# Storing the first-stage gate blocks raw, with their silu moved to the channel stage, and a new place for the residual's first tile

## The chip, the cores and the metric

The kernel runs on one core of one Trainium2 chip. The metric is the device time of one execution in microseconds (us). Engines are named as in the profile: PE is TensorE's matrix multiply and PEld its weight load, DVE is VectorE, ACT is ScalarE, POOL is GpSimd, and SP is the engine whose queue issues every transfer (DMA) of this kernel. L405 is line 405 of the kernel before.

## The reference

The kernel computes two layers of a hybrid decoder on a sequence of 1024 tokens of width 1024, in float32. One layer is:

```
h    = rms_norm(x, norm_g)
proj = h @ w_in
q_lat, kv_lat, k_rope, g_mla, c_h, c_b, c_c, g_conv, s_q, s_k, s_v, g_swa = split(proj)
y_mla  = mla_mixer(q_lat, kv_lat, k_rope, ...)   * silu(g_mla)     # latent attention, causal
y_conv = c_b * causal_conv3(c_c * c_h)           * silu(g_conv)    # short depthwise convolution
y_swa  = swa_mixer(s_q, s_k, s_v, ..., sinks)    * silu(g_swa)     # window of 128, softmax with sinks
x      = x + concat(y_mla, y_conv, y_swa) @ w_out
```

The change touches `silu(g_mla)`, the values that are kept until the latent attention is done, and the start of `x + ... @ w_out`.

## The kernel before

Every float32 product is made as three matmuls of a split pair (a rounded high part and the rest): high by high, high by low, low by high. `mm3` writes out these three for each block of 128 of the contraction, at L188, L189 and L190. Weights are loaded raw and split into such pairs (L171 makes the high part, L173 the low part; L551 and L552 in the channel stage). A buffer named `wraw` holds a raw piece, `whi` and `wlo` the pair; there are three raw buffers and eight pairs.

A layer runs in these stages, one behind the other on TensorE:

- **First stage.** The window attention runs in 16 steps (two halves of heads by eight blocks of 128 tokens). A step makes scores, masks them on VectorE (L353), takes exp on ScalarE (L358), scales on GpSimd (L364), transposes (L374), copies (L375) and multiplies with the values (L384). Between its parts the function `fill` puts other units: eight `unit_b` and eight `unit_a` (latents; the lists `P1_FILL` say how many at each step), then the gate blocks `unit_m`: a 128 by 512 block of `g_mla`, transposed, goes through silu on ScalarE (L405) into a buffer `gt` and by a transfer into the DRAM buffer `gm_d` (L406). Six of the eight `unit_m` of a layer run in this stage. The pool `p1` holds its tiles; `ali`, the mask of 4 KB per partition, is the first of them.
- **Channel stage.** The other two `unit_m` and the eight `unit_s` come first. Then the convolution's channels are made in four pairs of groups (`group_u` and `group_g`), each a scheme of seven products instead of eight (`seven`, L587) on sums and differences of quarters of the weights (`quarters`, with the tiles `a12` and `asum`) and of the input (`t_a`, `t_b`, `t_c`). The pool `cp` holds a ring of five buffers `st` of 2 KB per partition, `a12`, `asum` and three `yv`. `group_g` applies silu (L625), multiplies, and stores its result to DRAM as `ycv_d` (L649). DVE instructions of a group follow one another in a fixed order (`in_turn`). The last group calls two functions on the way (`beside`): `split_y` splits the window attention's result (blocks 4 to 7) and the convolution's (blocks 0 to 3) into the pairs `yh` and `yl` (L674, L676). Blocks 0 to 2 are loaded back from `ycv_d` as `yr`; block 3 is still in `yv`.
- **Output stage.** `unit_o` multiplies the pairs with `w_out` in 32 units of 24 matmuls (L188 to L190, here on `whi`, `yh`), over three PSUM buffers, and adds the residual tile `xr` (L723). `load_x` loads four blocks of it at a time into a ring of three buffers of 4 KB (tag `pt`) of the pool `at`, whose memory lies where `cp` was. From the unit numbered 9 on, `lat_t` transposes the latents (L741), which were stored to `lat_d` in the first stage and are loaded back by one transfer of 1.66 MB (L703).
- **Attention stage.** The latent attention runs in the same way with exp (L933), multiplies its rows by the stored gate (`gm`, loaded from `gm_d` during the output stage), and the last product and the next layer's norm follow.

The order of instructions on each engine is made by the framework's planner: it takes the program in the order in which it is written as priority, keeps a timeline of its own, and puts on each engine what is ready by that timeline. Within `tc.issue_after(i)` an instruction is put behind `i` on the same engine. A tile that reuses memory of a closed pool waits for the tiles that lay there (`reuse_waits="tile"`). An engine, and the SP queue, takes its instructions in order, so a wait holds all that is behind it.

Of the kernel before, what the change touches and what calls it, by code (L numbers as in the profile page):

```python
# [10 lines left out]
F32 = mybir.dt.float32  # L11
# [8 lines left out]
P = 128  # L20
# [43 lines left out]
def f32(ap):  # L64
    return ap.bitcast(F32)
# [3 lines left out]
def trunk(ctx, tc, x, norm_g, w_in, w_qb, w_kvb, w_out, c_gain, c_rope, c_idb, c_ali, out):  # L69
# [115 lines left out]
    def mm3(o, pairs):  # L185
        n = len(pairs)
        for i, (lh, ll, rh, rl) in enumerate(pairs):
            pe.matmul(o, lhsT=lh, rhs=rh, start=(i == 0), stop=False)  # L188
            pe.matmul(o, lhsT=lh, rhs=rl, start=False, stop=False)  # L189
            pe.matmul(o, lhsT=ll, rhs=rh, start=False, stop=(i == n - 1))  # L190

# [52 lines left out]
    for l in range(depth):  # L244
# [157 lines left out]
        def unit_m(w, k, hf, tmp):  # L402

            gt = tmp()
            s.activation(out=gt, in_=chan_mm(w, k % 2 * P, hf), func=AF.Silu)  # L405
            nc.sync.dma_start(out=gm_d[:, k, hf * 512:hf * 512 + 512], in_=gt)  # L406

        def unit_s(w, k, hf, tmp):
# [29 lines left out]
        units += [(lambda t=t: unit_a(t, W["a"])) for t in range(NT)]  # L438
        tmp = [lambda: p1.tile([P, 512], F32, name="gt", tag="gt", bufs=1)]
        for f, o in ((unit_m, O_GM), (unit_s, O_GS)):  # L440
            for jj in range(2):
                units += [(lambda f=f, k=2 * jj + c, hf=hf: f(W["gate"], k, hf, tmp[0])) for hf in (1, 0) for c in range(2)]
        after = {NT - 1: ("a", [win[:, :, O_QL:O_QL + QL], win[:, :, O_KR:O_KR + RD]])}
# [55 lines left out]

        tmp[0] = st  # L500
        tt = [a16(f"T{n}", FR).rearrange("p (b k q) -> p b k q", b=2, k=4) for n in range(3)]
# [7 lines left out]

        def whole(n, k):  # L510
            return sub(st(), f32(qx[n][0][:, k]), f32(qx[n][1][:, k]), ALU.add)

# [5 lines left out]
        def t_a(k):  # L518
            a, b = whole(4, k), whole(1, k)
            t2[k] = a, sub(b, a, b)  # L520
            t_split(5, k, b)
# [114 lines left out]
        def group_g(j, beside=(), e=g):  # L636
            yv = [cp.tile([P, 512], F32, name="yv", tag="yv", bufs=3) for _ in range(2)]
            kept.update(enumerate(yv))
            for hf in range(2):
                conv(j, hf, yv[hf])  # L640

            def times(hf, a, e):
                if e is v:
                    in_turn(yv[hf], a, yv[hf], ALU.mult)
                else:
                    e.tensor_tensor(out=yv[hf], in0=a, in1=yv[hf], op=ALU.mult)

            def store(hf):
                nc.sync.dma_start(out=ycv_d[:, j, hf * 512:hf * 512 + 512], in_=yv[hf])  # L649

            def last(o, a):
                times(1, plus(o, a), e)
                store(1)

            def c21(o, a):
                times(0, silu(o, a), e)
                store(0)

            seven(O_CB + j * P, O_GC + j * P, lambda o: times(0, o, v), c21, lambda o, a: times(1, silu(o, a), e), last, None, beside)
# [31 lines left out]
        for f, j in ((group_g, 0), (group_u, 1), (group_g, 1), (group_u, 2), (group_g, 2), (group_u, 3)):  # L691
            f(j)
        marks["turn"] = None
        group_g(3, (lambda: split_y(0, range(4, 8)), lambda: split_y(0, range(4))), v)

# [5 lines left out]
        kr = latf[:, NT * 384:NT * 416].rearrange("p (t c) -> p t c", t=NT)  # L701
        with tc.issue_after(marks["raw"].ins):
            nc.sync.dma_start(out=latf[:, :NT * 416], in_=lat_d)  # L703
        close(cp_cm)
# [7 lines left out]
        def load_x(qd, hf):  # L712
            xq[qd, hf] = at.tile([P, 4, 256], F32, name="xr", tag="pt", bufs=3)
            cs = slice(qd * 256, qd * 256 + 256)
            nc.sync.dma_start(out=xq[qd, hf], in_=xin[hf * 512:hf * 512 + 512, cs].rearrange("(t p) c -> p t c", p=P))

        def unit_o(qd, t, w):
            o = ps_g()[:, :256]
            hf, c = t // 4, (t % 4) * P
            yh, yl = y12[hf]  # L720
            mm3(o, [(yh[:, k, c:c + P], yl[:, k, c:c + P], *w[k]) for k in (4, 5, 6, 7, 0, 1, 2, 3)])
            xr = xq[qd, hf]
            v.tensor_tensor(out=xr[:, t % 4], in0=o, in1=xr[:, t % 4], op=ALU.add)  # L723
            if t % 4 == 3:
                cs = slice(qd * 256, qd * 256 + 256)
                nc.sync.dma_start(out=x1p[hf * 512:hf * 512 + 512, cs].rearrange("(t p) c -> p t c", p=P), in_=xr)
# [10 lines left out]
        def lat_t(k, hf):  # L737
            gn = kag[:, l:l + 1] if k == 2 else qag[:, l, k:k + 1]
            tp = ps_t()
            for c in range(4):  # L740
                pe.transpose(tp[:, c * P:(c + 1) * P], lat[:, hf * 4 + c, k * P:(k + 1) * P], idn)  # L741
            dst = slice(hf * 512, hf * 512 + 512)
# [269 lines left out]
        for i in range(4):  # L1012
            start += [lambda i=i: k1(0, i), lambda i=i: q1(0, 2 * i), lambda i=i: q1(0, 2 * i + 1), lambda i=i: k2(0, i)]
        load_x(0, 0)
        w1, wlp, wl, xTn, last = None, [], [], {}, []
# [181 lines left out]
```

## Time and the profile before

| | us |
|---|---|
| median of 3 runs (lowest, highest) | 1598.77 (1594.41, 1599.61) |
| the profiled execution | 1596.56 |
| its span, from the first to the last instruction | 1594.7 |

The profile and its trace are of that one execution. Busy time is summed per engine; TensorE's matmuls are pipelined, so a busy TensorE is not one at its peak. Idle time before an instruction is put down to the instruction that released it. PEclk is the granted clock of TensorE as a share of the full one. Of the stretches in the rows below, 65 to 260 lies in the first stage of layer 0 (its gate blocks from 164 on), 313 to 460 in its channel stage, 460 to 485 at the turn to its output stage; 850 to 1060 and 1246 to 1272 are the like places of layer 1.

### The profile page before, as it was taken

To read this page: it belongs to the slowest core of one execution; us is meant where nothing else is said; L and a number is where in the kernel's file an instruction comes from. 1 tells how busy PE (TensorE), PEld (TensorE's weight loads), DVE (VectorE), ACT (ScalarE), POOL (GpSimd) and SP (SyncE) were. 2 spreads that over 40 slices of the span, in tenths; PEclk is the share of its full clock that TensorE was granted. 3 is DMA by queue.
4 is the path that set the end of the run, shared out by engine and by line. 5 is a ranking of instruction groups with operands and counts; after the bars stand their busy time and mean duration, and the time that the engine had idled before them with its cause. 6 is when DMAs were issued, how large, how long until landed. Compare 5 with 4: busy or idle time off the path is not lost.

```text
span 1594.7 us, 25470 instructions
## 1 busy us (share of the span) xinstructions
PE 1495.8 (94%) x9084; PEld 1319.6 (83%) x9084; DVE 1102.9 (69%) x2197; ACT 739.9 (46%) x1763; POOL 734.8 (46%) x960
## 2 busy tenths in 40 slices
PE   6899988999999999999989998899999899999998
PEld 5898877788879998888778897778888799888887
DVE  6765565876774668887656755668667756788964
ACT  4353554422230258886524445644222302688851
POOL 6444231544434655874245423314444356568640
PEclk9999999999999999999999999999999999999999
DMA  6100222122246610013241102211222564100123
GB/s 203 34 10 21 83 67 60 27 60 64 82 139 209 208 51 2 1 41 121 79 134 33 29 1 81 75 54 39 70 77 60 190 206 152 47 1 14 47 75 131
DMA packets 116641, 122.73 MB, mean 77 GB/s; under 512 B 16417, under 2 KB 102305, under 8 KB 115746
## 3 DMA queue, kind: packets, MB, share of 16 engines
q1 hardware_dynamic: 116514, 121.10, 24.7%
q8 instruction: 72, 1.18, 0.3%
q14 instruction: 55, 0.45, 0.1%
HBM read 92.50 MB, written 28.57 MB: 76 GB/s over the span
## 4 chain that ended last, share of the span: by engine, by line
PE 74%; DVE 8%; ACT 8%; issue 4%; DMA 3%; POOL 3%; SPq 0%; POOLq 0%; ACTq 0%; DVEq 0%
PE ps_g L188 13%; PE ps_g L189 12%; PE ps_g L190 12%; PE ps_b L587 8%; PE ps_a L587 5%; PE ps_c L587 5%; PE ps_s L920 4%; PE ps_g L964 4%; PE ps_s L349 2%; ACT apr L933 2%; PE ps_g L384 2%; PE ps_t L950 1%; PE ps_t L374 1%; DVE pt L959 1%; DMA wraw<-in_w_in_dram 1%
## 5 line engine op out<-in xcount | busy, mean ns | idle before, releaser
L173 POOL TENSOR_TENSOR wlo<-wraw,whi 128x512 fp32r<-128x512 f32 (+2 forms) x120 | 164.8, 1380 | 134.5 <-DVE whi L171 98.8
L188 PE MATMUL ps_g<-whi,xh 128*128 128x320 f32 (+2 forms) x512 | 161.3, 315 | 5.9 <-ACT pr L358 1.8
L190 PE MATMUL ps_g<-whi,xl 128*128 128x320 f32 (+2 forms) x512 | 159.3, 311 | 0.0
L189 PE MATMUL ps_g<-wlo,xh 128*128 128x320 f32 (+2 forms) x512 | 159.2, 311 | 0.0
L190 PE MATMUL ps_g<-whi,yl 128*128 128x256 f32 x512 | 146.9, 287 | 5.6 <-DVE yl L676 5.6
L188 PE MATMUL ps_g<-whi,yh 128*128 128x256 f32 x512 | 147.6, 288 | 3.3 <-DVE xr L723 2.8
L189 PE MATMUL ps_g<-wlo,yh 128*128 128x256 f32 x512 | 145.9, 285 | 0.0
L964 PE MATMUL ps_g<-pt,vs 128*128 128x256 f32 (+1 forms) x640 | 120.6, 300 | 13.9 <-DVE pt L959 8.9
L364 POOL TENSOR_SCALAR pr<-pr,sri 128x256 f32<-128x256 f32 (+1 forms) x128 | 59.0, 479 | 140.7 <-DVE sri L362 108.7
L171 DVE CAST whi<-wraw 128x512 fp32r<-128x512 f32 (+2 forms) x128 | 82.0, 647 | 48.6 <-DMA wraw<-in_w_out_dram 22.5
L964 PEld LDWEIGHTS ps_g<-pt,vs 128*128 128x128 f32 x640 | 91.4, 190 | 25.6 <-DVE pt L959 15.1
L959 DVE TENSOR_TENSOR pt<-ps_t,pt 128x512 fp32r<-128x512 f32 (+1 forms) x160 | 100.2, 632 | 16.1 <-ACT pt L958 13.9
L188 PEld LDWEIGHTS ps_g<-whi,xh 128*128 128x128 f32 x512 | 102.4, 200 | 7.6 <-issue 2.7
L920 PE MATMUL ps_s<-kt,qh 96*128 96x512 f32 (+3 forms) x384 | 106.2, 361 | 0.9
L936 POOL TENSOR_SCALAR apr<-apr,ari 128x896 f32<-128x896 f32 (+2 forms) x80 | 71.7, 896 | 75.2 <-DVE ari L935 64.0
L190 PEld LDWEIGHTS ps_g<-whi,yl 128*128 128x128 f32 x512 | 99.2, 194 | 7.0 <-DVE yl L676 7.0
L188 PEld LDWEIGHTS ps_g<-whi,yh 128*128 128x128 f32 x512 | 99.3, 194 | 5.1 <-DVE xr L723 4.1
L189 PEld LDWEIGHTS ps_g<-wlo,xh 128*128 128x128 f32 x512 | 102.0, 199 | 1.6
L924 DVE TENSOR_REDUCE am<-ps_s 128x1 f32<-128x128 f32 (+7 forms) x128 | 95.6, 750 | 9.5 <-PE ps_s L922 7.1
L190 PEld LDWEIGHTS ps_g<-whi,xl 128*128 128x128 f32 x512 | 101.7, 199 | 0.4
L958 ACT CAST pt<-ps_t 128x512 fp32r<-128x512 f32 (+1 forms) x160 | 85.7, 542 | 35.2 <-PE ps_g L190 17.9
L188 PE MATMUL ps_g<-xh,whi 128*128 128x512 f32 x256 | 101.0, 395 | 0.0
(245 smaller groups left out, 4503.0 us busy)
## 6 DMA issues: line engine op xcount, KB each, us to landing
wraw<-in_w_in_dram SPq DMA_DIRECT2D x104, 256.0 KB, 2.9
wraw<-in_w_out_dram SPq DMA_DIRECT2D x80, 256.0 KB, 3.0
x1p<-xr SPq DMA_DIRECT2D x16, 512.0 KB, 3.2
p<-x1p SPq DMA_DIRECT2D x16, 512.0 KB, 3.5
x<-in_x_dram SPq DMA_DIRECT2D x8, 512.0 KB, 5.1
a<-in_w_in_dram SPq DMA_DIRECT2D x16, 256.0 KB, 3.4
ycv_d<-yv SPq DMA_DIRECT2D x16, 256.0 KB, 2.7
xr<-in_x_dram SPq DMA_DIRECT2D x8, 512.0 KB, 4.7
```

The lines of the kernel that those rows point to most:

```text
L171: cast(out=hi, in_=raw)
L173: e.tensor_tensor(out=lo, in0=raw, in1=f32(hi), op=ALU.subtract)
L188: pe.matmul(o, lhsT=lh, rhs=rh, start=(i == 0), stop=False)
L189: pe.matmul(o, lhsT=lh, rhs=rl, start=False, stop=False)
L190: pe.matmul(o, lhsT=ll, rhs=rh, start=False, stop=(i == n - 1))
L587: pe.matmul(o, lhsT=a[:, k], rhs=b[:, k], start=(first and k == 0 and i == 0), stop=(k == 3 and i == 2), skip_group_check=True)
L920: pe.matmul(sp[:, kk], lhsT=a[:, hs], rhs=kt[0:QK, b, h, kk], start=(ai == 0), stop=(ai == 2 and c0 + w < n))
L924: v.tensor_reduce(out=m, in_=sp[:, :n], axis=AX.X, op=ALU.max)
L936: g.tensor_scalar(out=pr[:, :n], in0=pr[:, :n], scalar1=ri, scalar2=1.0, op0=ALU.mult, op1=ALU.mult)
L958: s.copy(out=pt[:, 0, lo_c:], in_=tp[:, lo_c:])
L959: v.tensor_tensor(out=pt[:, 1, lo_c:], in0=tp[:, lo_c:], in1=f32(pt[:, 0, lo_c:]), op=ALU.subtract)
L964: pe.matmul(av[:, q0:], lhsT=vb, rhs=pt[:, a, q * 256 + q0:(q + 1) * 256], start=(bb == 0 and bi == 0 and a == 0), stop=(last and bi == 1 ...
```

## The change

`unit_m` copies a gate block raw while the first stage runs and notes it in the list `m_raw`; once the channel stage's buffers exist it applies silu as before. The new function `silu_m` loads one noted block from `gm_d` into a buffer of the ring `st`, applies silu in place, and stores it back; it is called once behind each of six groups of the channel stage. `a12` and `asum` become the first tiles of the pool `cp`: they are made ahead of everything else in it, and the first `t_a` uses them for its two sums. The first `load_x` is called as soon as the pool `at` is open, ahead of every other tile of it, so that its tile is the first there; the load of the latents is put behind it. The transposes of `lat_t` are put behind the last matmul of the latest `unit_o` (`mm3` now returns it). The convolution's block 3 is no longer stored to `ycv_d`. The first of the two functions beside the last group now also splits blocks 0 and 1, the second blocks 2 and 3.

```diff
--- before.py
+++ after.py
@@ -187,7 +187,8 @@
         for i, (lh, ll, rh, rl) in enumerate(pairs):
             pe.matmul(o, lhsT=lh, rhs=rh, start=(i == 0), stop=False)
             pe.matmul(o, lhsT=lh, rhs=rl, start=False, stop=False)
-            pe.matmul(o, lhsT=ll, rhs=rh, start=False, stop=(i == n - 1))
+            r = pe.matmul(o, lhsT=ll, rhs=rh, start=False, stop=(i == n - 1))
+        return r
 
     def rsqrt(name, ss, w, scale, eps):
         g.tensor_scalar(out=ss, in0=ss, scalar1=scale, scalar2=eps, op0=ALU.mult, op1=ALU.add)
@@ -402,8 +403,21 @@
         def unit_m(w, k, hf, tmp):
 
             gt = tmp()
-            s.activation(out=gt, in_=chan_mm(w, k % 2 * P, hf), func=AF.Silu)
+            o = chan_mm(w, k % 2 * P, hf)
+            if len(tmps) > 1:
+                s.activation(out=gt, in_=o, func=AF.Silu)
+            else:
+                s.copy(out=gt, in_=o)
+                m_raw.append((k, hf))
             nc.sync.dma_start(out=gm_d[:, k, hf * 512:hf * 512 + 512], in_=gt)
+
+        def silu_m():
+            k, hf = m_raw.pop(0)
+            gt = st()
+            blk = gm_d[:, k, hf * 512:hf * 512 + 512]
+            nc.sync.dma_start(out=gt, in_=blk)
+            s.activation(out=gt, in_=gt, func=AF.Silu)
+            nc.sync.dma_start(out=blk, in_=gt)
 
         def unit_s(w, k, hf, tmp):
 
@@ -436,10 +450,11 @@
 
         units = [(lambda t=t: unit_b(t, W["b"])) for t in range(NT)]
         units += [(lambda t=t: unit_a(t, W["a"])) for t in range(NT)]
-        tmp = [lambda: p1.tile([P, 512], F32, name="gt", tag="gt", bufs=1)]
+        m_raw = []
+        tmps = [lambda: p1.tile([P, 512], F32, name="gt", tag="gt", bufs=1)]
         for f, o in ((unit_m, O_GM), (unit_s, O_GS)):
             for jj in range(2):
-                units += [(lambda f=f, k=2 * jj + c, hf=hf: f(W["gate"], k, hf, tmp[0])) for hf in (1, 0) for c in range(2)]
+                units += [(lambda f=f, k=2 * jj + c, hf=hf: f(W["gate"], k, hf, tmps[-1])) for hf in (1, 0) for c in range(2)]
         after = {NT - 1: ("a", [win[:, :, O_QL:O_QL + QL], win[:, :, O_KR:O_KR + RD]])}
         for n, o in enumerate((O_GM, O_GM + 256, O_GS, O_GS + 256)):
             after[2 * NT - 1 + 4 * n] = n, [win[:, :, o:o + 256]]
@@ -497,7 +512,7 @@
             return cp.tile([P, 512], F32, name="st", tag="st", bufs=5)
 
 
-        tmp[0] = st
+        tmps.append(st)
         tt = [a16(f"T{n}", FR).rearrange("p (b k q) -> p b k q", b=2, k=4) for n in range(3)]
         qx = {n: tuple(x[:, 4 * j:4 * j + 4] for x in xT[hf]) for n, j, hf in ((1, 0, 0), (2, 1, 0), (3, 1, 1), (4, 0, 1))}
         qx.update((5 + n, (t[:, 0], t[:, 1])) for n, t in enumerate(tt))
@@ -507,8 +522,10 @@
             v.tensor_tensor(out=o, in0=a, in1=b, op=op)
             return o
 
-        def whole(n, k):
-            return sub(st(), f32(qx[n][0][:, k]), f32(qx[n][1][:, k]), ALU.add)
+        def whole(n, k, tmp=st):
+            return sub(tmp(), f32(qx[n][0][:, k]), f32(qx[n][1][:, k]), ALU.add)
+
+        ab = [cp.tile([P, 512], F32, name=t, tag=t, bufs=1) for t in ("a12", "asum")]
 
         def t_split(n, k, f):
             h, lo = (x[:, k] for x in qx[n])
@@ -516,7 +533,7 @@
             sub(lo, f, f32(h))
 
         def t_a(k):
-            a, b = whole(4, k), whole(1, k)
+            a, b = (whole(n, k, (lambda: ab.pop(0)) if ab else st) for n in (4, 1))
             t2[k] = a, sub(b, a, b)
             t_split(5, k, b)
 
@@ -646,7 +663,8 @@
                     e.tensor_tensor(out=yv[hf], in0=a, in1=yv[hf], op=ALU.mult)
 
             def store(hf):
-                nc.sync.dma_start(out=ycv_d[:, j, hf * 512:hf * 512 + 512], in_=yv[hf])
+                if j < 3:
+                    nc.sync.dma_start(out=ycv_d[:, j, hf * 512:hf * 512 + 512], in_=yv[hf])
 
             def last(o, a):
                 times(1, plus(o, a), e)
@@ -690,8 +708,10 @@
         group_u(0, w)
         for f, j in ((group_g, 0), (group_u, 1), (group_g, 1), (group_u, 2), (group_g, 2), (group_u, 3)):
             f(j)
+            if m_raw:
+                silu_m()
         marks["turn"] = None
-        group_g(3, (lambda: split_y(0, range(4, 8)), lambda: split_y(0, range(4))), v)
+        group_g(3, (lambda: split_y(0, (4, 5, 6, 7, 0, 1)), lambda: split_y(0, (2, 3))), v)
 
         split_y(1, range(4, 8))
         split_y(1, range(4))
@@ -699,8 +719,6 @@
         latf = a16("lat", F32)
         lat = latf[:, :NT * 384].rearrange("p (t c) -> p t c", t=NT)
         kr = latf[:, NT * 384:NT * 416].rearrange("p (t c) -> p t c", t=NT)
-        with tc.issue_after(marks["raw"].ins):
-            nc.sync.dma_start(out=latf[:, :NT * 416], in_=lat_d)
         close(cp_cm)
         psum_plan(1, 3, 3)
         uc_cm.__exit__(None, None, None)
@@ -712,13 +730,17 @@
         def load_x(qd, hf):
             xq[qd, hf] = at.tile([P, 4, 256], F32, name="xr", tag="pt", bufs=3)
             cs = slice(qd * 256, qd * 256 + 256)
-            nc.sync.dma_start(out=xq[qd, hf], in_=xin[hf * 512:hf * 512 + 512, cs].rearrange("(t p) c -> p t c", p=P))
+            marks["x"] = nc.sync.dma_start(out=xq[qd, hf], in_=xin[hf * 512:hf * 512 + 512, cs].rearrange("(t p) c -> p t c", p=P))
+
+        load_x(0, 0)
+        with tc.issue_after(marks["x"].ins):
+            nc.sync.dma_start(out=latf[:, :NT * 416], in_=lat_d)
 
         def unit_o(qd, t, w):
             o = ps_g()[:, :256]
             hf, c = t // 4, (t % 4) * P
             yh, yl = y12[hf]
-            mm3(o, [(yh[:, k, c:c + P], yl[:, k, c:c + P], *w[k]) for k in (4, 5, 6, 7, 0, 1, 2, 3)])
+            marks["o"] = mm3(o, [(yh[:, k, c:c + P], yl[:, k, c:c + P], *w[k]) for k in (4, 5, 6, 7, 0, 1, 2, 3)])
             xr = xq[qd, hf]
             v.tensor_tensor(out=xr[:, t % 4], in0=o, in1=xr[:, t % 4], op=ALU.add)
             if t % 4 == 3:
@@ -737,8 +759,9 @@
         def lat_t(k, hf):
             gn = kag[:, l:l + 1] if k == 2 else qag[:, l, k:k + 1]
             tp = ps_t()
-            for c in range(4):
-                pe.transpose(tp[:, c * P:(c + 1) * P], lat[:, hf * 4 + c, k * P:(k + 1) * P], idn)
+            with tc.issue_after(marks["o"].ins):
+                for c in range(4):
+                    pe.transpose(tp[:, c * P:(c + 1) * P], lat[:, hf * 4 + c, k * P:(k + 1) * P], idn)
             dst = slice(hf * 512, hf * 512 + 512)
             s.mul(lh[:, k, dst], tp, gn)
             v.scalar_tensor_tensor(out=ll[:, k, dst], in0=tp, scalar=gn, in1=f32(lh[:, k, dst]),
@@ -1011,7 +1034,6 @@
         start = []
         for i in range(4):
             start += [lambda i=i: k1(0, i), lambda i=i: q1(0, 2 * i), lambda i=i: q1(0, 2 * i + 1), lambda i=i: k2(0, i)]
-        load_x(0, 0)
         w1, wlp, wl, xTn, last = None, [], [], {}, []
         p4q, p4t, n_t = [], [], [0] * 4
         k2q = []
```

## Rows read from the trace of the kernel before

**Rows 1.** The page's first part: busy time, share of the span, instructions.
```profile
span 1594.7 us, 25470 instructions
...
PE 1495.8 (94%) x9084; PEld 1319.6 (83%) x9084; DVE 1102.9 (69%) x2197; ACT 739.9 (46%) x1763; POOL 734.8 (46%) x960
```

**Rows 2.** Stretches: start:end, length; each engine's busy us (instructions); granted clock, DMA share, GB/s.
```profile
65.00:160.00 95.00, 87.47 (x593) 82.21 (x593) 65.18 (x178) 43.44 (x145) 43.13 (x69) 0.96 0.11 28
160.00:260.00 100.00, 85.15 (x446) 73.82 (x445) 53.24 (x148) 56.09 (x140) 29.91 (x50) 0.90 0.20 64
...
313.00:460.00 147.00, 146.73 (x647) 121.56 (x648) 104.72 (x130) 41.01 (x70) 65.82 (x50) 1.00 0.25 68
460.00:485.00 25.00, 18.97 (x113) 16.36 (x113) 18.82 (x30) 9.85 (x17) 5.54 (x4) 0.93 0.78 264
...
850.00:960.00 110.00, 101.14 (x692) 95.54 (x691) 76.33 (x205) 51.98 (x174) 45.48 (x79) 0.95 0.09 23
960.00:1060.00 100.00, 89.42 (x461) 74.63 (x462) 56.92 (x144) 56.15 (x128) 29.56 (x46) 0.97 0.26 78
...
1246.00:1272.00 26.00, 19.04 (x113) 16.42 (x111) 18.32 (x29) 9.85 (x17) 5.63 (x5) 0.93 0.75 254
```

**Rows 3.** ScalarE's groups: line, operation, count; busy us, mean ns; idle before and releaser.
```profile
L405 ACT ACT_TABLE_LOAD x12 | 15.4, 1283 | 5.2 <-issue 5.0
L358 ACT ACT_TABLE_LOAD x10 | 12.8, 1283 | 19.5 <-DVE ses L356 19.4
...
L388 ACT COPY otmp<-ps_g 64x256 f32<-64x256 f32 x32 | 11.8, 369 | 29.7 <-PE ps_g L384 29.1
L625 ACT ACTIVATE st<-st 128x512 f32<-128x512 f32 x16 | 10.1, 632 | 28.5 <-DVE st L573 28.5
L593 ACT COPY st<-ps_a 128x512 f32<-128x512 f32 x16 | 9.3, 580 | 10.1 <-PE ps_a L587 10.1
```

**Rows 4.** The chain that ended last: start, us, what; table loads, first and last of seven.
```profile
166.76 1.28 ACT L358
...
1037.71 1.28 ACT L358
```

**Rows 5.** ScalarE in order of time, at the first gate block: start, us, what.
```profile
164.02 1.28 ACT L405 ACT_TABLE_LOAD   x1
165.31 0.60 ACT L405 ACTIVATE gt<-ps_g 128x512 f32<-128x512 f32 x1
```

**Rows 6.** TensorE in order of time at both turns, waiting rows; idle before in brackets.
```profile
470.99 0.38 PE L190 MATMUL ps_g<-whi,yl 128*128 128x256 f32 x1 [2.47 <-DVE yl L676]
...
481.68 1.53 PE L741 MATMUL ps_t<-idn,lat 128*128 128x128 f32 x12 [0.90 <-DMA lat<-lat_d]
484.62 0.39 PE L188 MATMUL ps_g<-whi,yh 128*128 128x256 f32 x1 [1.41 <-DVE xr L723]
...
1257.53 0.39 PE L190 MATMUL ps_g<-whi,yl 128*128 128x256 f32 x1 [2.35 <-DVE yl L676]
...
1269.11 1.53 PE L741 MATMUL ps_t<-idn,lat 128*128 128x128 f32 x12 [2.42 <-DMA lat<-lat_d]
1272.04 0.38 PE L188 MATMUL ps_g<-whi,yh 128*128 128x256 f32 x1 [1.40 <-DVE xr L723]
```

**Rows 7.** VectorE and the DMA queue in order of time, layer 0's turn.
```profile
469.17 2.96 DVE L676 TENSOR_TENSOR yl<-yr,yh 128x512 fp32r<-128x512 f32 x3
...
476.97 2.87 SPq L715 DMA_DIRECT2D xr<-in_x_dram  x3
...
484.14 1.09 DVE L723 TENSOR_TENSOR xr<-ps_g,xr 128x256 f32<-128x256 f32 x3 [5.39 <-DMA xr<-in_x_dram]
```

**Rows 8.** VectorE, then TensorE in order of time, last group of layer 0's channel stage.
```profile
447.37 0.68 DVE L552 TENSOR_TENSOR wlo<-asum,whi 128x512 fp32r<-128x512 f32 x1
...
463.96 0.39 PE L587 MATMUL ps_c<-xh,whi 128*128 128x512 f32 x1
```

**Rows 9.** The page's DMA issues: count, KB each, us to landing.
```profile
wraw<-in_w_in_dram SPq DMA_DIRECT2D x104, 256.0 KB, 2.9
```

## The prediction

> **What bounds the kernel now.** I read the page first. TensorE is busy for 94% of the span [rows 1], so only two things can shorten the run much: fewer TensorE instructions, or less of the 99 us in which TensorE stands still. The change removes no matmul, so it can gain only from that 99 us. The table of stretches says where it lies [rows 2]. The first stage of layer 0 idles 7.5 us of 95 before its gate blocks begin (65 to 160) and 14.9 us of 100 while they run (160 to 260); in layer 1 it is 8.9 of 110 and 10.6 of 100. The channel stage (313 to 460) idles 0.3 us of 147: there everything off TensorE is hidden. The turn to the output stage idles 6.0 us of 25 in layer 0 and 7.0 us of 26 in layer 1.
>
> Next I read the ScalarE groups [rows 3]. The activation-table loads of this stage are 12 at the silu line of the gate blocks and 10 at the softmax's exp: in the first stage the engine swaps silu and exp for each of six gate blocks per layer. A load takes 1.283 us; the silu itself 0.60 us [rows 5]. The chain that ended last shows how many of these loads are on the path [rows 4]: seven, five in layer 0 and two in layer 1; the first and the last are shown. The other 15 lie beside TensorE work. Last I read the turn itself in order of time [rows 6, 7].
>
> **Part 1: silu out of the first stage.** Six gate blocks per layer are copied instead of passed through silu. A copy of such a block from PSUM is 0.580 us [rows 3] against 0.60, which is nothing. Copies between exps need no load of their own: the copy of `otmp` stands in the same steps as the exps, 32 times, and has no load at its line [rows 3]. So the six silu loads shrink to one per layer (the seventh block, in the channel stage) and the five exp loads of each layer vanish: 2 x (5 + 5) = 20 of 22. Only those on the path count: 7 x 1.283 = 9.0 us. A second way gives the same size: if the stretches with gate blocks idled at the share of the stretches before them, layer 0 would save 14.9 - 7.9 = 7.0 us and layer 1 10.6 - 8.1 = 2.5 us, together 9.5. What is late next is the rest of the attention chain, which idles TensorE at about 8% without any load. Ends: 0, if that chain fills every gap, and 20 x 1.283 = 25.7. I take 9.0, the row-by-row count.
>
> The trace shows no cost beside the load: it begins at 164.02, and the silu behind it starts at 165.31, 1.29 us later [rows 5]. The Trainium skill, "ScalarE: Activation LUTs", section "What ACT_TABLE_LOAD costs", has the same 1283 ns for the load and adds about 1380 ns of draining for every switch, some 2.66 us. By that page the seven switches would be an estimated 18.6 us; by the row they are 9.0. I go by the row, since 10 ns separate load and silu there.
>
> **Part 2: silu in the channel stage.** Per layer six loads of 256 KB, six silus of 0.632 us [rows 3] and six stores. ScalarE is busy 41 of 147 us there [rows 2], and 6 x 0.632 = 3.8 us fit into that; these silus stand among silus and bring no table load. The DMA engines are 25% busy there [rows 2]. What could hurt is order, since one queue (SP) issues all transfers: a store that waits for its silu holds back the weight loads behind it. One block costs at most a load, about 2.9 us for the same size [rows 9], plus 0.6 us of silu, so 3.5 us. The cover is the lead of the weights: the last weight subtraction that reads `asum` ends at 448.05, and the product that uses it starts at 463.96, 15.9 us later [rows 8]. So the weights are early, not late. I take 0. Without that cover it would be 12 x 3.5 = 42 us. The `st` ring (5 buffers) gives one more buffer per group; a group takes three and lasts some 19 us (147 us for the eight), so a ring slot is long free: 0. The two stores of block 3 that go away shorten only the queue: 0. `t_a(0)` writing to `a12` and `asum` only gives two VectorE results another place, written in the same order: 0.
>
> **Part 3: the residual's first tile.** Now the first `xr` load is issued at 476.97, once the splits of `y` have freed the memory under it, and VectorE gets it at 484.14 [rows 7]. TensorE has only three PSUM buffers for the output units, so the fourth unit waits 1.41 us for it, and 0.90 us go to the latent's transposes, which the schedule pulled up and which wait for their load; in layer 1 it is 1.40 and 2.42 [rows 6]. After the change `xr` is the first tile of its pool and lies on `a12` and `asum`, which are free from 448.05 on [rows 8]. It can be issued up to 29 us sooner, and with a landing of 7.2 us (476.97 to 484.14) it is there before unit 0 ends even if it is issued at 465. It passes the latent's load, four `w_out` pieces and the small `idb` load on SP; these are needed later (nine units on for the latent), and the transposes are tied behind an output unit, so they can't wait in front of one. They keep their 1.53 us of TensorE time. Gain: 0.90 + 1.41 + 1.40 + 2.42 = 6.1 us; ends 0 and 6.1. What is late next is `yl`.
>
> **Part 4: two splits sooner.** Unit 0 stops 2.47 us (layer 1: 2.35) for `yl` [rows 6]. Three subtractions on loaded blocks run back to back for 2.96 us from 469.17 [rows 7], held behind the last chain of block 3. Two of them are now allowed earlier, behind the chain before. At 0.99 us each that is at most 2.0 us per layer, and nothing if they delay that last chain, which block 3 needs. I take half: 1.9 us over both layers; ends 0 and 3.9. The granted clock of both turns is 0.93 [rows 2], it falls after that wait; 7% of 51 us is 3.6 us at most that could come back, and I count none.
>
> **Sum.** -9.0 - 6.1 - 1.9 = -17.0 us. The profiled execution took 1596.56 us, so 1579.6; the median of the runs is 2.2 us above it, so 1581.8. I forecast 1582 us, -1.05%.
>
> **Rivals.** (a) The loads were on the path only in name: the wait for exp becomes one for POOL's scaling of `pr` or VectorE's masking, and the first stage gives nothing. For it: the stretches without gate blocks idle 8% too. Against: layer 0 idles twice that share exactly where the loads are. 1598.8 - 8.0 = 1591. (b) The turn gives nothing, because the splits of `y` on VectorE, busy 18.8 of 25 us there [rows 2], take the place of `xr`. Against: VectorE idles 5.39 us before the first `xr` row [rows 7]. 1598.8 - 9.0 = 1590. (c) Slower: the stores of the 12 blocks hold SP and the weights come late, 42 us against 17 gained, 1624. It decides only once the queue is held for more than the 15.9 us lead within a group of 19 us; one 3.5 us hold per group doesn't reach that. (d) The change does nothing that shows: instructions are ordered by a planner with its own times, and another order in the first stage gives back what the loads gave and the turn keeps its waits: 1597. (e) A switch costs an emptied engine besides its load. It would double part 1, 1598.8 - 18 - 8 = 1573. The 10 ns of [rows 5] speak against it. The Trainium skill, "ScalarE: Activation LUTs", section "What ACT_TABLE_LOAD costs", has this as its rule.
>
> **How the numbers follow.** Forecast 0.57, its own range 1572 to 1588; (a) 0.16; (b) 0.10; (c) 0.06; (d) 0.08; (e) 0.03. The range reaches to (a), (b) and (e): 1571 to 1593, which leaves out (c), (d) and small tails. About 0.3% (4.8 us) is what a measurement of this kernel can tell from no change. Faster by more than that: the forecast, (a), (b), (e), 0.86; within it (d), 0.08; slower (c), 0.06.
>
> **What the profile would show.** Right: two table loads at the silu lines, none at the exp line of the first stage; idle of the two gate stretches near 8%; `xr` landed before unit 0 ends, no wait of a transpose for `lat`; the channel stage idling under 1 us per layer. Wrong: table loads among the exps, a new wait for `pr` or `sy` of the same length, a wait for weights in the channel stage, or the output units waiting for `yl` 5 us instead of 2.4.

## The result and the profile after

The changed kernel takes 1572.03 us (median of 4 runs, 1569.59 to 1572.78), the kernel before, measured beside it, 1596.59 (4 runs): a ratio of 0.9843, 95% interval 0.9818 to 0.9867, 24.6 us less. The forecast stands at 1582 us and 17.0 us of gain, with a range of 1571 to 1593: the direction is right, and the time falls 1 us above the lower end. So there is more gain than the sum has terms for, and the traces have to say where.

The page's first part for the kernel after, to be held against [rows 1]: TensorE has the same 9084 matmuls and 7.0 us less busy time, ScalarE 18.3 us less. TensorE's idle time, the span less its busy time, falls from 98.9 to 82.2 us. These 16.7 us are near the forecast's 17.0; the 7.0 us of busy time come on top.

```profile
span 1571.0 us, 25506 instructions
...
PE 1488.8 (95%) x9084; PEld 1317.0 (84%) x9084; DVE 1104.3 (70%) x2197; ACT 721.6 (46%) x1755; POOL 737.6 (47%) x960
```

The two traces can't be compared at equal times, since everything behind a gain comes sooner. So the stretches below begin and end at the same instruction in each kernel: the two gate stretches at ScalarE's exp of the sink sums (`ses`) of the 9th and the 16th attention step in layer 0, the 10th and the 16th in layer 1; the third line lies within layer 0's channel stage. Columns as in [rows 2]; kernel after:

```profile
160.26:239.83 79.57, 71.06 (x406) 62.22 (x404) 51.78 (x141) 37.98 (x117) 27.15 (x45) 0.96 0.23 75
941.92:1020.73 78.81, 71.89 (x396) 61.97 (x395) 48.80 (x129) 35.54 (x108) 29.77 (x44) 0.96 0.25 79
301.00:447.00 146.00, 145.98 (x644) 120.89 (x645) 104.47 (x129) 43.92 (x75) 64.63 (x50) 1.00 0.31 90
```

The same two gate stretches of the kernel before:

```profile
161.07:252.93 91.86, 78.14 (x415) 69.03 (x414) 50.22 (x141) 51.12 (x128) 27.09 (x45) 0.89 0.20 65
957.51:1040.82 83.31, 74.12 (x401) 62.91 (x399) 48.61 (x129) 48.42 (x118) 29.65 (x44) 0.96 0.24 75
```

Three things are to be seen. Layer 0's gate stretch is 12.3 us shorter, layer 1's 4.5. In layer 0 idle time gives only 5.2 of these (91.86 - 78.14 = 13.72 before, 8.51 after); TensorE's busy time falls by 7.1, and its granted clock rises from 0.89 to 0.96 (nine matmuls fewer lie between the two marks, so not all of the 7.1 is clock). And the channel stage idles 0.02 us of 146 with its new loads, silus and stores. From its first product to its last it takes 153.19 us in layer 0 both before and after.

ScalarE's groups after, columns as in [rows 3]: the gate blocks are copies (L410), two table loads are left at the channel stage's silu line (L408), and L359, the softmax's exp, has none. The 16.2 us that ScalarE waits for the blocks loaded back (L419) reach no matmul.

```profile
L419 ACT ACTIVATE st<-st 128x512 f32<-128x512 f32 x12 | 7.5, 629 | 16.2 <-DMA st<-gm_d 16.2
L410 ACT COPY gt<-ps_g 128x512 f32<-128x512 f32 x12 | 7.1, 588 | 14.0 <-PE ps_g L190 6.6 <-issue 6.5 <-ACT ses L361 0.7
...
L408 ACT ACT_TABLE_LOAD x2 | 2.6, 1283 | 0.0
```

The turn of layer 0 after, which answers to [rows 6, 7]. TensorE's waiting rows first, all there are between 455 and 490; then the queue SP, VectorE's splits, and GpSimd's subtractions for the low parts of the output weights:

```profile
457.21 0.38 PE L190 MATMUL ps_g<-whi,yl 128*128 128x256 f32 x1 [0.59 <-DVE yl L694]
...
459.82 0.58 PE L190 MATMUL ps_g<-whi,yl 128*128 128x256 f32 x1 [1.99 <-DVE yl L694]
...
461.02 0.58 PE L190 MATMUL ps_g<-whi,yl 128*128 128x256 f32 x1 [0.19 <-DVE yl L694]
```

```profile
459.68 0.46 SPq L733 DMA_DIRECT2D xr<-in_x_dram  x1
460.24 0.45 SPq L737 DMA_DIRECT2D lat<-lat_d  x1
```

```profile
454.07 0.67 DVE L694 TENSOR_TENSOR yl<-yr,yh 128x512 fp32r<-128x512 f32 x1
...
455.61 1.55 DVE L694 TENSOR_TENSOR yl<-yr,yh 128x512 fp32r<-128x512 f32 x1
...
458.02 1.75 DVE L694 TENSOR_TENSOR yl<-yr,yh 128x512 fp32r<-128x512 f32 x1
```

```profile
455.31 1.30 POOL L173 TENSOR_TENSOR wlo<-wraw,whi 128x512 fp32r<-128x512 f32 x1 [4.72 <-DVE whi L171]
457.63 1.59 POOL L173 TENSOR_TENSOR wlo<-wraw,whi 128x512 fp32r<-128x512 f32 x1 [1.02 <-issue]
```

The waits for `xr` and `lat` are gone, though `xr` is not issued until 459.68. The wait for `yl` is still there: 2.77 us in three pieces.

### The profile page after: what moved, and what is told of

It reads as the page before. It is cut to its first block, busy times and chain, and to the rows that moved or that the text cites. A ratio compares the mean times of both kernels' runs of the same rounds, so it can differ in the third digit from the quotient of the medians.

```text
span 1571.0 us, 25506 instructions
## 1 busy us (share of the span) xinstructions
PE 1488.8 (95%) x9084; PEld 1317.0 (84%) x9084; DVE 1104.3 (70%) x2197; ACT 721.6 (46%) x1755; POOL 737.6 (47%) x960
## 4 chain that ended last, share of the span: by engine, by line
PE 75%; DVE 8%; ACT 7%; issue 4%; POOL 3%; DMA 2%; SPq 0%; POOLq 0%; ACTq 0%; DVEq 0%
PE ps_g L188 13%; PE ps_g L190 13%; PE ps_g L189 13%; PE ps_b L604 8%; PE ps_a L604 6%; PE ps_c L604 5%; PE ps_s L943 4%; PE ps_g L987 4%; DMA wraw<-in_w_in_dram 2%; PE ps_s L350 2%; ACT apr L956 2%; PE ps_g L385 2%; PE ps_t L973 1%; PE ps_t L375 1%; POOL wlo L173 1%
## 5 line engine op out<-in xcount | busy, mean ns | idle before, releaser
L189 PE MATMUL ps_g<-xl,whi 128*128 128x512 f32 x256 | 100.5, 393 | 0.0
```

## The experiments

Two theories of the surplus start out. By the one, it is the table loads: one that makes an exp late stops TensorE and also leaves it at a lower granted clock, so the loads are worth more than those on the chain. By the other, it is the order: the planner puts other instructions first in the changed stages, and the loads are worth no more than the chain says. Each run is compared with the kernel before on the same chip (medians 1597.82, 1595.09 and 1596.36 us in the three groups of runs).

**1. Only the table loads away (b_copy), and the change in halves.** The kernel before, with Copy for silu in the six gate blocks of a layer's first stage, nothing else (these blocks stay raw):

```diff
-            s.activation(out=gt, in_=chan_mm(w, k % 2 * P, hf), func=AF.Silu)
+            s.activation(out=gt, in_=chan_mm(w, k % 2 * P, hf), func=AF.Silu if hasattr(tmp, "late") else AF.Copy)
...
-        tmp[0] = st
+        tmp[0], st.late = st, True
```

> The kernel before with one word changed: the six gate blocks per layer of the first stage are copied instead of passed through silu, and nothing puts the silu back, so their gates are left raw (the output is another). The order of instructions on every engine is that of the kernel before, less 20 table loads on ScalarE. If the first stage's gain comes from the loads alone, all of it is here: about 19 us less than before (12 in layer 0, 7 in layer 1), 9 from idle time and the rest because TensorE's clock stays up. If the planner's other order made it, only the seven loads counted on the path show: 9 us or less. If each switch cost 2.66 us, as the page says, 7 on the path would give 18.6 with no change of the clock.

gate_only has the raw store and `silu_m` of the change and the old turn:

> The kernel before with the gate part alone: blocks stored raw, loaded back, silu applied and stored in the channel stage. Loads theory: the same as with the copy alone, 19 us less than before, and the channel stage as long as it was (147.1 us in layer 0). If the silus in the channel stage cost something on the queue or on ScalarE: up to 3.5 us for each of 12 blocks given back, so less gain than the copy alone by a few us.

turn_only is the changed kernel with the silu back in the first stage:

```diff
-            o = chan_mm(w, k % 2 * P, hf)
-            if len(tmps) > 1:
-                s.activation(out=gt, in_=o, func=AF.Silu)
-            else:
-                s.copy(out=gt, in_=o)
-                m_raw.append((k, hf))
+            s.activation(out=gt, in_=chan_mm(w, k % 2 * P, hf), func=AF.Silu)
```

> The changed kernel with silu back in the first stage: only the turn to the output stage differs from before. Theory: the waits for xr and for the latents go (6.1 us), but the remaining wait for yl keeps the clock low for longer, so 4 to 6 us less than before. Rival (the turn gives nothing): within 2 us of before. Rival (the turn gives what was forecast): 8 us.

place_only is gate_only with `a12` and `asum` first in their pool, `load_x(0, 0)` moved, and the latents' load behind it; the old order of splits, no tie of the transposes, block 3 still stored:

> The gate part and, of the turn, only the place and time of the residual's first tile (and the latents' load behind it); the transposes are not tied, the splits stay as they were, block 3 is still stored. Theory: the wait for xr (1.4 us per layer) goes, but transposes pulled up still wait for the latents, whose load now starts later: 1 to 3 us less than the gate part alone. Rival (place is all of the turn's gain): 5 us less than the gate part alone.

| kernel | median, us | ratio (95%) | against before |
|---|---|---|---|
| b_copy | 1579.88 | 0.9885 (0.9867 to 0.9904) | -17.9 |
| gate_only | 1581.53 | 0.9900 (0.9883 to 0.9917) | -16.3 |
| turn_only | 1589.51 | 0.9949 (0.9935 to 0.9964) | -8.3 |
| place_only | 1572.56 | 0.9851 (0.9831 to 0.9871) | -25.3 |

The halves add up: 16.3 + 8.3 = 24.6, the whole change; by their intervals they are 13.3 to 18.7 and 5.8 to 10.4 us. b_copy has on every engine the order of before, less 20 table loads on ScalarE. It gains 17.9 us, so no change of order is needed for this part. Its gate stretch in layer 0 and, in TensorE's order of time, the scores behind the first gate block:

```profile
160.49:240.05 79.56, 71.05 (x406) 62.22 (x405) 51.70 (x141) 37.98 (x118) 27.49 (x45) 0.96 0.23 75
```

```profile
167.85 1.22 PE L349 MATMUL ps_s<-sx 128*128 128x256 f32 x8 [2.36 <-ACT pr L358]
```

The same scores in the kernel before:

```profile
170.04 2.08 PE L349 MATMUL ps_s<-sx 128*128 128x256 f32 x8 [3.93 <-ACT pr L358]
```

The wait for exp is 1.57 us longer with the loads, a little more than one load. And the eight matmuls behind it take 2.08 us instead of 1.22: they wait longer, and then they run slower. The stretch from 164 to 174 us shows it as the granted clock (a mean over its two levels of 1.2 and 2.4 GHz), 0.75 in before and 1.00 in b_copy, with 30 matmuls against 55. One such place does not show a price, since the clock also falls without loads: tiny_square of experiment 2, which has none here, is at 0.83 in the same stretch. Before, then b_copy:

```profile
164.00:174.00 10.00, 6.07 (x30) 5.49 (x30) 5.94 (x22) 6.50 (x16) 2.51 (x6) 0.75 0.57 222
```

```profile
164.00:174.00 10.00, 7.64 (x55) 7.14 (x54) 6.36 (x25) 6.08 (x23) 2.06 (x5) 1.00 0.53 216
```

**2. Loads put back into the changed kernel without their work.** A one-column activation behind each raw copy: Silu, which swaps tables against exp, or Square, which doesn't.

```diff
                 s.copy(out=gt, in_=o)
                 m_raw.append((k, hf))
+                tz = small.tile([P, 1], F32, name="tz")
+                s.activation(out=tz, in_=gt[:, 0:1], func=AF.Silu)
```

> The changed kernel plus one silu of 128 x 1 behind each of the six raw copies per layer, its result unused. It brings the 20 table loads back into the first stage and nothing else: next to the run with a square of 128 x 1 in its place, the order on every engine is the same but for the loads. Loads theory: about 16 us slower than the run with the square, most of it between the 9th and the 16th step of each layer, and the granted clock of layer 0's gate stretch back from 0.96 to about 0.89. Rival (the gain was the planner's other order): within 3 us of it.

> The control of the run with the tiny silu: a square of 128 x 1 (no table load of its own) behind each raw copy. Loads theory: the changed kernel's time, 1572 us, within 3. Rival: the extra instruction itself costs.

tiny_silu takes 1591.74 us (0.9970, 0.9956 to 0.9983), tiny_square 1572.30 (0.9848, 0.9832 to 0.9863). The order of both is the same but for the loads, 23 against 5. So 18 loads cost 19.4 us, 1.08 us each in the mean. They don't cost alike: from one step's exp of the sink sums to the next one's, a step with two of the loads is 0.34 to 4.04 us longer. I had expected 16 us for 20 loads. TensorE's line of the two pages, tiny_silu (span 1590.0 us) and then tiny_square (1570.7):

```profile
PE 1495.7 (94%) x9084; PEld 1321.4 (83%) x9084; DVE 1100.5 (69%) x2197; ACT 745.9 (47%) x1785; POOL 733.2 (46%) x960
```

```profile
PE 1484.8 (95%) x9084; PEld 1312.7 (84%) x9084; DVE 1106.5 (70%) x2197; ACT 721.9 (46%) x1767; POOL 735.2 (47%) x960
```

Of the 19.3 us between the spans, 8.4 are idle time of TensorE (94.3 against 85.9 us) and 10.9 are busy time, for the same matmuls in the same order. The idle part is near the 9.0 us that the chain of before gives for its seven loads; the other part is no wait at all. Layer 0's gate stretch, tiny_silu and then tiny_square:

```profile
158.39:250.22 91.83, 77.47 (x412) 68.26 (x411) 49.53 (x141) 51.66 (x132) 27.05 (x45) 0.89 0.20 65
```

```profile
158.69:240.07 81.38, 71.92 (x409) 63.37 (x408) 50.45 (x141) 38.59 (x123) 27.41 (x45) 0.96 0.23 73
```

Of the 10.45 us, idle time is 4.9 us (14.36 against 9.46) and busy time 5.55 (77.47 against 71.92), for three matmuls more; busy time by granted clock is 77.47 x 0.89 = 68.9 and 71.92 x 0.96 = 69.0. It is the same work at a lower clock. About half of what the loads cost in this stretch is clock, and a chain shows that part as matmuls. In layer 1 it is 8.4 us, and the clock falls there too; tiny_silu, then tiny_square:

```profile
953.22:1039.28 86.06, 75.63 (x401) 64.87 (x399) 48.48 (x129) 46.40 (x121) 29.68 (x44) 0.92 0.23 72
```

```profile
942.68:1020.36 77.68, 70.60 (x396) 60.78 (x395) 49.09 (x129) 35.84 (x113) 29.70 (x44) 0.98 0.26 80
```

Rival (e) has another account of the surplus: a drained engine at every switch. ScalarE of tiny_silu in order of time, at its first swap:

```profile
163.32 1.28 ACT L413 ACT_TABLE_LOAD   x1
164.61 0.20 ACT L413 ACTIVATE tz<-gt 128x1 f32<-128x1 f32 x1
...
164.83 1.28 ACT L359 ACT_TABLE_LOAD   x1
166.13 0.47 ACT L359 ACTIVATE pr<-ps_s,snm 128x256 f32<-128x256 f32 x1
```

The silu starts 10 ns behind its load and the exp 20 ns behind the other. ScalarE shows no emptied stretch. The Trainium skill, "ScalarE: Activation LUTs", section "What ACT_TABLE_LOAD costs", gives the 1283 ns of the load, which these rows show, and some 1380 ns of drain for each switch, which they don't. By its 2.66 us the seven loads of [rows 4] would cost an estimated 18.6 us, near the measured gain; the rows show that the gain comes by another way.

**3. The silus in the channel stage (no_late_silu).** The changed kernel without `silu_m`: twelve gate blocks stay raw, and their loads, silus and stores are left out.

```diff
-            if m_raw:
-                silu_m()
```

> The changed kernel without the function that loads the raw blocks back, applies silu and stores them: six gates per layer stay raw (the output is another). If the silus in the channel stage are hidden, as forecast, the changed kernel's time within 2 us, 1572, and the channel stage at 153.2 us in layer 0 as in every run so far. If they cost something: up to 3.5 us for each of 12 blocks less, 1530 at the least.

It takes 1571.79 us (0.9845, 0.9826 to 0.9863), against 0.9843 with them. b_copy and gate_only, which differ by the same silus, are 1.7 us apart with overlapping intervals. Part 2 costs nothing that these runs can tell.

**4. The splits (late_splits).** The changed kernel with the splits of `y` in their old batches:

```diff
-        group_g(3, (lambda: split_y(0, (4, 5, 6, 7, 0, 1)), lambda: split_y(0, (2, 3))), v)
+        group_g(3, (lambda: split_y(0, range(4, 8)), lambda: split_y(0, range(4))), v)
```

> The changed kernel with the splits of y in their old two batches (blocks 4 to 7, then 0 to 3). Forecast's step: the earlier splits of blocks 0 and 1 give 1.9 us over both layers, so 1574. What the run with the place alone suggests: they give nothing, 1572 within 2, because the wait moves from block 0 to block 2.

It takes 1571.40 us (0.9847, 0.9830 to 0.9863): the earlier splits are worth nothing. Its turn in layer 0, VectorE, TensorE's waiting rows, and a stretch of 21.88 us around the end of the channel stage:

```profile
454.42 1.28 DVE L171 CAST whi<-wraw 128x512 fp32r<-128x512 f32 x1
...
456.38 2.96 DVE L694 TENSOR_TENSOR yl<-yr,yh 128x512 fp32r<-128x512 f32 x3
```

```profile
458.18 0.38 PE L190 MATMUL ps_g<-whi,yl 128*128 128x256 f32 x1 [2.49 <-DVE yl L694]
...
460.59 0.58 PE L190 MATMUL ps_g<-whi,yl 128*128 128x256 f32 x1 [0.19 <-DVE yl L694]
```

```profile
447.32:469.20 21.88, 18.53 (x113) 16.45 (x112) 19.45 (x32) 8.01 (x14) 5.87 (x5) 0.92 0.73 250
```

The same stretch of the changed kernel, which is 0.6 us behind by then:

```profile
447.32:469.20 21.88, 18.44 (x99) 16.28 (x98) 18.63 (x29) 8.11 (x14) 5.70 (x5) 0.84 0.74 254
```

The waits for `yl` are 2.68 us here and 2.77 in the changed kernel, whose clock is the lower one. There the first of the three splits starts 2.3 us sooner, 2.9 counted from the last channel product (453.63 here, 454.21 there). But unit 0 needs the third split too, and before that one ends VectorE has the same seven instructions to run in either order, one right behind the other: the three splits, two casts of output weights and two steps of block 3's chain. They take 5.84 us here (from 453.49) and 5.70 there (from 454.07). GpSimd's two subtractions lengthen VectorE's work by some 2 us in both: here a cast (1.28 us; one takes 0.41 alone) and one of the splits, there two splits, so that the three take 3.97 us instead of 2.96.

**5. Two units begun before one is finished (two_units).** If `yl` of blocks 2 and 3 is what is late, the first two output units should both do the other six blocks first:

```diff
+        def head_o(t, w):
+            part_o[t] = ps_g()[:, :256]
+            with tc.issue_after(marks["o"].ins) if "o" in marks else nullcontext():
+                mm_o(t, w, (4, 5, 6, 7, 0, 1), part_o[t])
...
+            if (qd, t) in ((0, 0), (0, 1)):
+                o = part_o[t]
+                mm_o(t, w, (2, 3), o)
```

> The changed kernel, with the first two output units cut: each does its six early blocks (4 to 7, 0, 1), and only then do both do blocks 2 and 3. This puts 18 matmuls (2.1 us) of the second unit in front of the matmul that now waits 2.0 us for yl of block 2. If the wait and the low clock behind it are what is left at the turn: 2 to 3 us of waiting and about 2 us of clock less per layer, so 4 to 10 us less than the changed kernel, about 1565. Rival (VectorE's order there is the limit and another wait follows): within 2 us of 1572.

It takes 1567.62 us (1565.31 to 1568.02; 0.9816, 0.9802 to 0.9830), less than before and after the change; late_splits beside it took 1571.40, 3.8 us more. What waits in its turn:

```profile
456.12 0.38 PE L747 MATMUL ps_g<-whi,yl 128*128 128x256 f32 x1 [0.59 <-DVE yl L694]
...
459.96 0.39 PE L747 MATMUL ps_g<-whi,yl 128*128 128x256 f32 x1 [0.58 <-DVE yl L694]
...
465.71 0.39 PE L745 MATMUL ps_g<-whi,yh 128*128 128x256 f32 x1 [1.78 <-DVE xr L763]
```

1.60 us of the wait for `yl` are gone, and a new one has come: a fourth unit waits 1.78 us for the addition to `xr`, which frees its buffer and which stands on VectorE behind the splits of the second half. So TensorE doesn't wait less. From the last channel product to the end of the third output unit, in layer 0 and layer 1, the changed kernel and then two_units:

```profile
454.21:473.87 19.66, 16.89 (x112) 16.15 (x111) 15.81 (x25) 4.70 (x8) 5.53 (x4) 0.83 0.72 248
1233.01:1252.44 19.43, 16.68 (x112) 15.92 (x111) 15.72 (x25) 4.25 (x7) 5.53 (x4) 0.82 0.71 250
```

```profile
453.12:471.77 18.65, 15.70 (x112) 14.98 (x111) 16.09 (x25) 4.57 (x8) 6.68 (x5) 0.91 0.76 265
1229.80:1246.99 17.19, 14.23 (x112) 13.51 (x111) 15.69 (x25) 4.28 (x8) 5.56 (x4) 1.00 0.79 276
```

Idle time is 2.77 and 2.75 us in the changed kernel, 2.95 and 2.96 in two_units; what is shorter is the busy time, at a higher clock. How much of it belongs to the edit is not shown: late_splits, as long as the changed kernel by medians, has 0.91 in both layers.

**6. Three of those splits on GpSimd (two_units_pool).** two_units, with this besides:

```diff
+                e = g if hf and 3 < k < 7 else v
...
-                    v.tensor_tensor(out=yl[:, k], in0=src, in1=f32(yh[:, k]), op=ALU.subtract)
+                    e.tensor_tensor(out=yl[:, k], in0=src, in1=f32(yh[:, k]), op=ALU.subtract)
```

> The run with two cut output units, with three of the eight splits of y's second half per layer on GpSimd instead of VectorE. What still waits there is the fourth unit, 1.8 us for VectorE's addition of xr, which stands behind these splits. If only VectorE's queue matters: the wait goes, 2 to 4 us less than 1567.6. If VectorE slows down beside GpSimd (its subtractions of 0.68 us took 1.55 to 1.78 while GpSimd subtracted), the splits left on VectorE take longer and nothing is gained, within 2 us or slower.

It takes 1572.08 us (0.9846, 0.9827 to 0.9865); the gain of two_units is gone. VectorE, then GpSimd, then TensorE at its turn:

```profile
450.62 3.59 DVE L695 TENSOR_TENSOR yl<-osw,yh 128x512 fp32r<-128x512 f32 x4
```

```profile
451.93 5.12 POOL L695 TENSOR_TENSOR yl<-osw,yh 128x512 fp32r<-128x512 f32 x3 [1.78 <-ACT yh L692]
```

```profile
459.43 0.39 PE L748 MATMUL ps_g<-whi,yl 128*128 128x256 f32 x1 [2.84 <-DVE yl L695]
...
468.93 0.39 PE L746 MATMUL ps_g<-whi,yh 128*128 128x256 f32 x1 [1.69 <-DVE xr L764]
```

The wait for `yl` has grown to 2.84 us: GpSimd's three splits slow what VectorE does beside them. Its four splits of the first half, of which only the last lies beside them, take 3.59 us, where the changed kernel has this row:

```profile
451.06 2.48 DVE L694 TENSOR_TENSOR yl<-osw,yh 128x512 fp32r<-128x512 f32 x4
```

The wait for `xr` is still 1.69 us, but its cause is another. VectorE is through with its splits sooner than it can add: it idles for the residual's transfer, which is issued 8.2 us behind the last channel product here, not 5.5:

```profile
468.45 1.09 DVE L764 TENSOR_TENSOR xr<-ps_g,xr 128x256 f32<-128x256 f32 x3 [1.62 <-DMA xr<-in_x_dram]
```

The same stretches as in experiment 5:

```profile
453.77:473.51 19.74, 14.49 (x112) 13.56 (x111) 16.59 (x24) 4.40 (x8) 8.81 (x6) 1.00 0.69 236
1232.74:1254.80 22.06, 17.09 (x112) 16.44 (x111) 17.41 (x24) 4.45 (x8) 9.92 (x7) 0.85 0.65 223
```

TensorE idles 5.25 and 4.97 us in them, 4.3 more than in two_units. In layer 0 the clock stays at 1.00 all the same, so a wait doesn't cost clock every time.

## Why the prediction was right, and where it was short

The measured time lies in the range, but at its very end: the forecast's own range begins at 1572, and 1571 was taken in for rival (e), whose mechanism the rows don't show. That the time still lies inside is in part luck.

**Part 1: the idle time was counted rightly, and a term was missing.** The step that failed is "The change removes no matmul, so it can gain only from that 99 us". Measured are 16.3 (gate_only) and 17.9 us (b_copy), where 7 x 1.283 = 9.0 us were forecast. The page of b_copy, whose span is 1578.4 us, to be held against [rows 1]:

```profile
PE 1488.9 (94%) x9084; PEld 1314.1 (83%) x9084; DVE 1108.5 (70%) x2197; ACT 714.1 (45%) x1743; POOL 737.0 (47%) x960
```

TensorE's idle time falls by 9.4 us, from 98.9 to 89.5, near the 9.0 that the chain named. Its busy time falls by 6.9 us besides, with the same matmuls in the same order. In the pair of experiment 2 the parts are 8.4 us idle and 10.9 busy. The prediction read the lower clock of 0.90 in this stretch [rows 2] and made no term of it; it counted idle time alone. Its cross-check by idle shares could not see the clock either, and so agreed with a sum that was short: in the gate stretches idle time fell by 5.2 us in layer 0 and 2.3 in layer 1, near the 7.0 and 2.5 of that check. In the two profiles of before and after, layer 1's gate stretch is at 0.96 both times, and gains 4.5 us where layer 0 gains 12.3. That isn't a property of the layer: in tiny_silu it is at 0.92, against 0.98 without the loads. Why its clock kept up in the profile of before is left open.

**Part 2: right**, for the reason given. The channel stage keeps its 153.19 us, and leaving the silus out changes nothing.

**Part 3: right.** 6.1 us of waits were counted. The waits for `xr` and for `lat` are gone in both layers, and no new one has come: TensorE's 2.77 and 2.75 us of idle time in the stretches of experiment 5 are the wait for `yl`. From the last channel product to the first cast of an attention tile (`pt`) the profiled turns of place_only are 2.7 us shorter in each layer than those of gate_only (112.22 against 114.93 and 112.38 against 115.07 us), 5.4 together. By medians place_only is 9.0 us under gate_only, and turn_only's interval is 5.8 to 10.4 us. Of the 8.7 us between the two profiled spans, another 3.1 lie in the gate stretches, where the two kernels idle alike and the clock is 0.96 in gate_only and 0.98 in place_only. No run shows these to be a gain of the turn. One detail was wrong: `xr` was to be issued up to 29 us sooner, near the end of `asum`'s last reader. It is issued 5.5 us behind the last channel product, where before it came 10.5 us behind. That was enough.

**Part 4: wrong, 1.9 us forecast, nothing measured.** The forecast took two of the three splits out of the wait, but unit 0 needs the third as well, and VectorE has as much to do before that one ends (experiment 4). The bound of "nothing if they delay" named another delay. Before, the last split of blocks 0 to 2 ends 5.67 us behind the last channel product (472.13 by [rows 7], the product starting at 466.46); after, 5.56 (459.77 and 454.21). The granted clock of the turn is 0.84, against 0.93 in [rows 2] and 0.92 in late_splits, so nothing of the 3.6 us that were left uncounted there shows as come back.

**The rivals.** (a) and (b) would have left one half at nothing, and each half gives its share alone. (c) is excluded by experiment 3, (d) by the result and by experiment 1. (e) named nearly the measured time, 1573, by a mechanism that the rows don't show. As measured the halves are 16.3 and 8.3 us, where the forecast had 9.0 and 8.0: nearly the whole shortfall is the price of the loads. That the turn comes out so near is partly luck, since part 4 gave nothing and the interval of turn_only is wide.

## What to carry to other kernels

Where an engine's short stall makes TensorE wait again and again, read the granted clock of that stretch beside its idle time, and price the stall by a pair of kernels that differ in it alone: the chain gave the idle part well here, but it books slow matmuls as matmuls. Table loads among the steps of a softmax are worth taking out even where the chain names only a few of them. Before an instruction is moved ahead on a full engine, count what must still be done before the last of its kind that is needed: here the order changed and the end did not. Moving late work to another engine helps only if the two don't share what they wait for.

## What the runs showed of the hardware that was not expected

- Table loads of 1.283 us among exps cost 1.08 us of the whole run each in the mean (18 loads, 19.4 us). Of the 19.3 us between the profiled spans 8.4 are idle time of TensorE and 10.9 longer busy time for the same matmuls; in layer 0's gate stretch the granted clock was 0.89 instead of 0.96.
- A wait didn't cost clock every time: at the turn of two_units_pool TensorE idled 5.25 us of 19.74 in layer 0 at a clock of 1.00, and 4.97 us of 22.06 in layer 1 at 0.85.
- VectorE's subtraction of 128x512 with both inputs in SBUF takes 0.67 us alone (454.07) and 1.55 and 1.75 us beside GpSimd's (455.61 and 458.02). The first overlaps it by 1.00 us and is 0.88 longer; the second overlaps by 1.20 us and is 1.08 longer. The Trainium skill, "SBUF — State Buffer", section "SBUF: two separate sides", says that a VectorE instruction with two SBUF inputs and a GpSimd instruction that reads SBUF need a shared pair of ports, which the one that starts first holds for its whole instruction while the other blocks. The rows agree: VectorE is longer by about the time of the overlap.
